# A hybrid decoder trunk on one core: first gate ahead of later weight splits, first rounds later, last conv tile by token halves

## The chip, the cores and the metric

The kernel runs on one core of one Trainium2 chip. The metric is device time in microseconds (us). The kernel before takes 1067.33 us (median of 3 runs, 1067.3 to 1068.85). TensorE is called PE, VectorE DVE, ScalarE ACT, GpSimd POOL, and SyncE, which issues most DMAs, SP. SBUF is the on-chip memory that all engines read; PSUM is the accumulator memory of PE, here eight banks of 128 x 512 floats.

## The reference

Two layers over 512 tokens of 1024 channels, in fp32. Layer A is a Conformer convolution module and a SwiGLU FFN, layer B attends over a shared K/V in a window of 128 and has an FFN too; a last RMSNorm follows. The change is about the first half of layer A (and, in one helper, about all RMSNorms):

```python
def rmsnorm(x, g):
    xf = x.astype(jnp.float32)
    xf = xf * lax.rsqrt(jnp.mean(xf * xf, axis=-1, keepdims=True) + EPS)
    return (xf * g.astype(jnp.float32)).astype(x.dtype)

def conformer_conv(x, w_pw1, b_pw1, w_dw, b_dw, ln_g, ln_b, w_pw2, b_pw2):
    a = jax.nn.glu(x @ w_pw1 + b_pw1, axis=-1)
    y = lax.conv_general_dilated(
        a, w_dw[:, None, :].astype(a.dtype), window_strides=(1,),
        padding=((CONV_WIDTH - 1, 0),),
        dimension_numbers=('NWC', 'WIO', 'NWC'),
        feature_group_count=D_MODEL) + b_dw
    y = jax.nn.silu(layernorm(y, ln_g, ln_b))
    return y @ w_pw2 + b_pw2
```

## The kernel before

Channels lie on partitions, tokens along the free dimension. An fp32 product is made of three products in a faster format: each operand is split in a high part (a cast) and a low part (the rest), and `mm3` (lines 345 to 347, in a fixed order `mm3_in_turn`, line 337) adds high·high, high·low and low·high in one bank. Weight chunks are split by ACT (`whi`) and DVE (`wlo`, both line 269). The chunks have numbers: pw1's tile ct has chunks 2·ct and 2·ct + 1, and `split_limit` and `held` say how far, and after which instruction, `split_chunk` may go.

The first stage ends at about 162 us. Its PE work is pw1 tile by tile (`project`): eight tiles ct of 128 channels, each with a linear and a gate bank and two halves of 24 products. RMSNorm's per-token factor is applied behind the product. It is made once (`Rms`): squares summed over channels, sums over partitions by PE, `ms` (DVE, line 435), `rs` by a power on POOL (line 437), then `diagonals` (DVE, line 452: identity times rs), which `spread` multiplies by a matrix of ones on PE, so that each partition has the row, and a copy to `rsbc` by ACT (line 447).

`gate` (lines 774 to 777) multiplies both banks by rsbc, takes a sigmoid and writes `apad`, the padded input of the depthwise convolution. Then SP stores apad to DRAM (`rowsd`, line 782) and loads it back four times, shifted (`shifted`, line 784). The 31 taps are shared by three engines: `products` (ACT multiplies, POOL adds, line 826), `taps` (a chain on DVE that sums in a PSUM bank, the last one into y, line 280) and `rounds` (PE products over 32-row blocks of `shifted` with diagonal `tables`, three to five rounds of four for each tile). DVE builds the tables in `round_weights` (line 712). `last` (DVE, line 843) joins PE's bank and y.

`inside(ct)` places other work between the products of tile ct: in tile 1 the sums, the spread and conv 0's gate; in tiles 2 to 5, after the first half, rounds and join of conv ct − 2. Behind the eighth tile stand the rounds of convs 4 to 6, then conv 7, which has four of its taps on PE by diagonal matrices (`diagonals` of `Conv`), then the sums for the LayerNorm (`sums`, `means`, `scales`), and the LayerNorm itself, which feeds pw2.

Banks come from a ring of eight in the order of the calls of `bank()`: a call waits for the last reader of the bank eight calls ago. `in_turn`, `Turn` and `issue_after` fix an order on an engine by hand; elsewhere a scheduler orders the instructions of each engine.

## Time and profile before

| what | value |
|---|---|
| median of three runs | 1067.33 us |
| profiled execution | 1066.32 us |
| its span | 1064.5 us |
| PE busy in the span | 1042.4 us (98%) |
| DVE, ACT, POOL busy | 71%, 47%, 17% |
| mean granted PE clock | 0.991 |
| first stage's end (first product of pw2) | 160.8 us |

Times in the trace count from the start of the span. A row of the timeline gives start and length of a run of alike instructions, engine, line and operation, the tile written and read, the shape, how many there were, and in brackets how long the engine had been idle and what ended that. A product in fp32 stands as two records, so 12 of them are x24.

### The profile page before, as it was taken

To read this page: it belongs to the slowest core of one execution; us is meant where nothing else is said; L and a number is where in the kernel's file an instruction comes from. 1 tells how busy PE (TensorE), PEld (TensorE's weight loads), DVE (VectorE), ACT (ScalarE), POOL (GpSimd) and SP (SyncE) were. 2 spreads that over 40 slices of the span, in tenths; PEclk is the share of its full clock that TensorE was granted. 3 is DMA by queue.
4 is the path that set the end of the run, shared out by engine and by line. 5 is a ranking of instruction groups with operands and counts; after the bars stand their busy time and mean duration, and the time that the engine had idled before them with its cause. 6 is when DMAs were issued, how large, how long until landed. Compare 5 with 4: busy or idle time off the path is not lost.

```text
span 1064.5 us, 15933 instructions
## 1 busy us (share of the span) xinstructions
PE 1042.4 (98%) x6404; PEld 893.5 (84%) x6404; DVE 759.7 (71%) x986; ACT 500.7 (47%) x764; POOL 182.0 (17%) x200
## 2 busy tenths in 40 slices
PE   8799999999999999999999999999999999999997
PEld 6466637888999899899988787788899988998996
DVE  7889837769786577658486767577978755776563
ACT  6565716434454254235463665354445522552353
POOL 0689810421000000000031342142100000000000
PEclk9899999999999999999999999999999999999999
DMA  7646568324234134221323211232423441243112
GB/s 252 176 141 160 139 141 118 99 84 154 80 100 159 40 106 143 89 80 61 119 79 99 80 41 41 80 99 79 139 79 102 131 145 40 99 141 97 41 60 79
DMA packets 36917, 111.62 MB, mean 105 GB/s; under 512 B 4395, under 2 KB 7260, under 8 KB 36828
## 3 DMA queue, kind: packets, MB, share of 16 engines
q1 hardware_dynamic: 35692, 109.32, 34.7%
q10 hardware_dynamic: 1152, 1.29, 0.3%
q8 instruction: 50, 0.82, 0.3%
q14 instruction: 23, 0.19, 0.1%
HBM read 106.25 MB, written 4.73 MB: 104 GB/s over the span
## 4 chain that ended last, share of the span: by engine, by line
PE 94%; DVE 2%; DMA 1%; issue 1%; ACT 1%; POOL 0%; SPq 0%; POOLq 0%; ACTq 0%; DVEq 0%
PE bank L337 24%; PE bank L345 23%; PE bank L346 23%; PE bank L347 22%; PE bank L1226 2%; DVE quad L470 1%; DMA shifted<-rowsd 1%; DVE wlo L269 0%; DMA rnd<-in_rnd_dram 0%; DVE tables L712 0%; DMA rowsd<-apad 0%; PE bank L1216 0%; PE bank L462 0%; PE bank L433 0%; ACT whi L269 0%
## 5 line engine op out<-in xcount | busy, mean ns | idle before, releaser
L346 PE MATMUL bank<-quad,whi 128*128 128x256 f32 (+1 forms) x1536 | 489.0, 320 | 1.3 <-DVE quad L470 0.9
L345 PE MATMUL bank<-quad,whi 128*128 128x256 f32 (+1 forms) x1536 | 483.2, 320 | 0.3 <-ACT tmp L617 0.3
L347 PE MATMUL bank<-quad,wlo 128*128 128x256 f32 (+1 forms) x1536 | 481.8, 319 | 0.0
L269 ACT CAST whi<-raw 128x1024 fp32r<-128x1024 f32 x174 | 182.3, 1050 | 296.6 <-PE bank L346 195.2
L346 PEld LDWEIGHTS bank<-quad,whi 128*128 128x128 f32 x1536 | 292.5, 190 | 23.5 <-DVE quad L470 1.3
L345 PEld LDWEIGHTS bank<-quad,whi 128*128 128x128 f32 x1536 | 291.2, 190 | 22.8 <-ACT quad L280 0.7
L347 PEld LDWEIGHTS bank<-quad,wlo 128*128 128x128 f32 x1536 | 290.0, 190 | 20.7 <-issue 0.5
L269 DVE TENSOR_TENSOR wlo<-raw,whi 128x1024 fp32r<-128x1024 f32 x174 | 221.3, 1275 | 110.7 <-ACT whi L269 99.6
L337 PE MATMUL bank<-quad,whi 128*128 128x512 f32 x512 | 162.3, 398 | 3.6 <-DVE quad L280 2.6
L337 PEld LDWEIGHTS bank<-quad,whi 128*128 128x128 f32 x512 | 95.6, 190 | 31.0 <-issue 5.3
L269 DVE TENSOR_TENSOR wlo<-blocks,whi 128x1024 fp32r<-128x1024 f32 x54 | 65.5, 1221 | 54.3 <-ACT whi L269 54.3
L337 PE MATMUL bank<-quad,wlo 128*128 128x512 f32 x256 | 100.3, 392 | 0.0
L269 ACT CAST whi<-blocks 128x1024 fp32r<-128x1024 f32 x54 | 56.6, 1048 | 86.8 <-PE bank L346 65.6
L826 POOL TENSOR_TENSOR quad<-quad 128x512 f32<-128x512 f32 x53 | 72.9, 1376 | 19.1 <-ACT quad L824 15.9
L337 PEld LDWEIGHTS bank<-quad,wlo 128*128 128x128 f32 x256 | 48.4, 189 | 10.4
L1237 POOL TENSOR_TENSOR rs<-ss,mhalf 128x1 f32<-128x1 f32 x4 | 2.2, 547 | 297.6 <-DVE ss L1235 297.6
L423 POOL TENSOR_TENSOR tmp<-tmp,tmp 128x512 f32<-128x512 f32 x21 | 32.9, 1566 | 113.1 <-ACT tmp L421 89.0
L1099 POOL COPY sc<-sk 128x4 f32<-128x4 f32 x16 | 3.5, 253 | 256.8 <-DVE wlo L269 254.6
L824 ACT ACTIVATE quad<-apad,wdw 128x512 f32<-128x512 f32 x53 | 36.6, 717 | 17.2 <-POOL quad L826 17.2
L499 DVE TENSOR_TENSOR h<-bank,h 128x512 f32<-128x512 f32 x56 | 37.1, 684 | 8.4 <-PE bank L347 8.4
L1123 POOL TENSOR_SCALAR sc<-sc,sm 128x256 f32<-128x256 f32 (+1 forms) x64 | 31.6, 514 | 66.0 <-DVE sm L1121 65.9
L1119 ACT ACTIVATE sc<-sc,m 128x257 f32<-128x257 f32 (+1 forms) x64 | 30.2, 475 | 22.2 <-DVE m L1110 22.2
(167 smaller groups left out, 1010.4 us busy)
## 6 DMA issues: line engine op xcount, KB each, us to landing
raw<-in_W_dram SPq DMA_DIRECT2D x139, 512.0 KB, 3.5
blocks<-in_W_dram SPq DMA_DIRECT2D x36, 512.0 KB, 4.5
shifted<-rowsd SPq DMA_DIRECT2D x16, 262.0 KB, 5.8
shifted<-rowsd SPq DMA_DIRECT2D x12, 260.0 KB, 5.3
rowsd<-apad SPq DMA_DIRECT2D x8, 271.0 KB, 2.5
bias<-fd SPq DMA_DIRECT2D x8, 256.0 KB, 10.2
h<-in_xT_dram SPq DMA_DIRECT2D x3, 512.0 KB, 7.1
shifted<-rowsd SPq DMA_DIRECT2D x4, 264.0 KB, 5.1
```

The costliest lines, as they stand in the source:

```text
L269: done = (nc.scalar.copy(hi, r).ins, lo_engine[0].tensor_sub(lo, r, f32(hi)).ins)
L337: turn[0] = nc.tensor.matmul(*args, **kw).ins
L345: nc.tensor.matmul(out, w[0], x[0], start=start, stop=False, **kw)
L346: nc.tensor.matmul(out, w[0], x[1], start=False, stop=False, **kw)
L347: nc.tensor.matmul(out, w[1], x[0], start=False, stop=stop, **kw)
L423: eng.tensor_add(sq, self.acc[eng], sq)
L499: nc.vector.tensor_add(t, banks[m], t)
L824: nc.scalar.mul(pr, src, self.tap(j))
L826: nc.gpsimd.tensor_add(to, acc, pr)
L1119: nc.scalar.activation(sc[:, j, 0:1 + w], sc[:, j, 0:1 + w], AF.Exp, bias=self.m4[:, j:j + 1], scale=-1.0, accum_out=sm[:, j:j + 1])
L1123: nc.gpsimd.tensor_scalar(sc[:, j, 1:1 + w], sc[:, j, 1:1 + w], sm[:, j:j + 1], 0.0, op0=ALU.mult, op1=ALU.add)
L1226: nc.tensor.matmul(self.banks[g], x, w[:, k, :], start=False, stop=kp == LAST[1] - 1 and k == 1 and n == 2)
```

## The change

Seven things change, all in the first stage but for the first:

1. `spread` takes the column of factors itself. Four products, each with one column repeated 128 times as the stationary side and the identity as the moving side, give what one product of ones by a diagonal matrix gave. `diagonals` and its DVE operation go, for all rms rows and for both LayerNorm rows.
2. The three tables built ahead of the first split of x are not built there. Four tables (0 to 3) are built between `ms` and the first gate, the other four after the gate of tile 1. There are nine warm-up products for seven.
3. Conv 0's gate comes ahead of the splits of chunks 5, 6 and 7, which are held until it has been issued.
4. Rounds and join of conv 0 move from the middle of tile 2 to its end; the position table and its rows move one tile later.
5. The DMAs of a gate are issued in the order of the code.
6. Conv 7 works in two banks by halves of 256 tokens: diagonal taps, rounds, join with y, copy, square and sums for each half.
7. `means` comes behind the first half's join.

On DVE, around conv 0's gate (`apad_334` before, `apad_329` after; tables, gate, and the splits `wlo` of chunks 5 to 7), before, from the row behind ms:

```order
L712 TENSOR_TENSOR tables_137<-eye,rnd 128x512
L712 TENSOR_TENSOR tables_138<-eye,rnd 128x384
L452 TENSOR_TENSOR tmp_308<-ident,rs_304 128x512
L712 TENSOR_TENSOR tables_138<-eye,rnd 128x512 x2
L712 TENSOR_TENSOR tables_138<-eye,rnd 128x640
L269 TENSOR_TENSOR wlo_322<-raw_215,whi_321 128x1024
L269 TENSOR_TENSOR wlo_438<-raw_241,whi_437 128x1024
L774 TENSOR_TENSOR tmp_336<-bank_212,rsbc_178 128x512
L776 TENSOR_TENSOR bank_211<-bank_211,rsbc_178 128x512
L774 TENSOR_TENSOR tmp_398<-bank_272,rsbc_178 128x512
L776 TENSOR_TENSOR bank_271<-bank_271,rsbc_178 128x512
L777 SCALAR_TENSOR_TENSOR apad_334<-bank_211,prm,tmp_336 128x512
```

and now:

```order
L435 TENSOR_SCALAR ms_301<-bank_296 128x4
L701 TENSOR_TENSOR tables_139<-eye,rnd 128x384
L701 TENSOR_TENSOR tables_139<-eye,rnd 128x512
L701 TENSOR_TENSOR tables_139<-eye,rnd 128x384
L701 TENSOR_TENSOR tables_139<-eye,rnd 128x512
L764 TENSOR_TENSOR tmp_331<-bank_211,rsbc_177 128x512
L766 TENSOR_TENSOR bank_210<-bank_210,rsbc_177 128x512
L764 TENSOR_TENSOR tmp_397<-bank_271,rsbc_177 128x512
L767 SCALAR_TENSOR_TENSOR apad_329<-bank_210,prm,tmp_331 128x512
L269 TENSOR_TENSOR wlo_344<-raw_214,whi_343 128x1024
L269 TENSOR_TENSOR wlo_441<-raw_240,whi_440 128x1024
L280 TENSOR_SCALAR bank_366<-apad_329,wdw 128x512
```

The line numbers are those of the changed kernel. The diagonal is gone, the tables ahead of the gate are four instead of five, and no split stands between ms and the gate. Behind it, on DVE, where conv 0's taps end and conv 1's begin, before:

```order
L280 TENSOR_SCALAR bank_367<-apad_334,wdw 128x512
L280 SCALAR_TENSOR_TENSOR bank_367<-apad_334,wdw,bank_367 128x512 x7
L280 SCALAR_TENSOR_TENSOR quad_132<-apad_334,wdw,bank_367 128x512
L280 TENSOR_SCALAR bank_423<-apad_396,wdw 128x512
L280 SCALAR_TENSOR_TENSOR bank_423<-apad_396,wdw,bank_423 128x512 x6
L280 SCALAR_TENSOR_TENSOR quad_132<-apad_396,wdw,bank_423 128x512
L269 TENSOR_TENSOR wlo_564<-raw_319,whi_563 128x1024
```

and now:

```order
L269 TENSOR_TENSOR wlo_471<-raw_272,whi_470 128x1024
L280 SCALAR_TENSOR_TENSOR bank_366<-apad_329,wdw,bank_366 128x512 x6
L280 SCALAR_TENSOR_TENSOR quad_134<-apad_329,wdw,bank_366 128x512
L280 TENSOR_SCALAR bank_422<-apad_395,wdw 128x512
L701 TENSOR_TENSOR tables_140<-eye,rnd 128x384
L701 TENSOR_TENSOR tables_140<-eye,rnd 128x512 x2
L701 TENSOR_TENSOR tables_140<-eye,rnd 128x640
L280 SCALAR_TENSOR_TENSOR bank_422<-apad_395,wdw,bank_422 128x512 x6
L269 TENSOR_TENSOR wlo_561<-raw_315,whi_560 128x1024
L280 SCALAR_TENSOR_TENSOR quad_134<-apad_395,wdw,bank_422 128x512
```

Four tables stand behind the first tap of conv 1, and a split between its last two taps. On PE, where rounds 0 stood in the middle of tile 2 (bank_434 and bank_433), before:

```order
L337 MATMUL bank_433<-quad_129,whi_275 128x512
L337 MATMUL bank_433<-quad_128,wlo_276 128x512
L337 MATMUL bank_465<-shifted_341,tables_137 32x512 x12
L337 MATMUL bank_434<-quad_130,whi_321 128x512
L337 MATMUL bank_434<-quad_131,whi_321 128x512
```

and now, between the last products of tile 2 and the first of tile 3:

```order
L337 MATMUL bank_436<-quad_132,whi_343 128x512
L337 MATMUL bank_436<-quad_133,whi_343 128x512
L337 MATMUL bank_436<-quad_132,wlo_344 128x512
L337 MATMUL bank_498<-shifted_336,tables_139 32x512 x12
L337 MATMUL bank_557<-quad_130,whi_440 128x512
L337 MATMUL bank_557<-quad_131,whi_440 128x512
```

On PE behind the last rounds of conv 6 (the sums alternate y and its square, and four rows like the two shown are left out), before:

```order
L337 MATMUL bank_1149<-shifted_1004,tables_138 32x512 x16
L337 MATMUL bank_1181<-apad_1088,quad_136 128x512 x4
L337 MATMUL bank_885<-quad_133,ones_m 32x512
L337 MATMUL bank_885<-quad_136,ones_m 32x512
L337 MATMUL bank_1197<-sel,tmp_1195 128x2 x4
L337 MATMUL bank_1181<-shifted_1095,tables_138 32x512 x16
L337 MATMUL bank_1181<-quad_133,ident 128x512
L337 MATMUL bank_1181<-shifted_1095,tables_138 32x512 x4
L337 MATMUL bank_1197<-sel,quad_133 128x1 x4
L337 MATMUL bank_1197<-sel,quad_136 128x1 x4
L337 MATMUL bank_1242<-quad_132,ones_m 128x512
```

and now:

```order
L337 MATMUL bank_1184<-apad_1091,quad_138 128x256 x4
L337 MATMUL bank_1185<-apad_1091,quad_138 128x256 x4
L337 MATMUL bank_888<-quad_135,ones_m 32x512
L337 MATMUL bank_888<-quad_138,ones_m 32x512
L337 MATMUL bank_1184<-shifted_1098,tables_140 32x256 x20
L337 MATMUL bank_1184<-quad_135,ident 128x256
L337 MATMUL bank_1226<-sel,tmp_1224 128x2 x4
L337 MATMUL bank_1226<-sel,quad_135 128x1 x2
```

```order
L337 MATMUL bank_1226<-sel,quad_138 128x1 x2
L337 MATMUL bank_1185<-shifted_1098,tables_140 32x256 x20
L337 MATMUL bank_1185<-quad_135,ident 128x256
L337 MATMUL bank_1226<-sel,quad_135 128x1 x2
L337 MATMUL bank_1226<-sel,quad_138 128x1 x2
L337 MATMUL bank_1273<-ident,mv_1265 128x128 x4
L337 MATMUL bank_1278<-quad_134,ones_m 128x512
L337 MATMUL bank_1280<-ident,rr_1268 128x128 x4
```

Each half has its own rounds, join and sums, and the `sel` products stand behind the first half's join.

```diff
-N_WARM = 7
+N_WARM = 9
...
-            had = nc.vector.tensor_scalar(ms, st[:, 0:4], 1.0 / D, EPS, op0=ALU.mult, op1=ALU.add).ins
+            self.had = nc.vector.tensor_scalar(ms, st[:, 0:4], 1.0 / D, EPS, op0=ALU.mult, op1=ALU.add).ins
             self.rs = small.tile([P, 4], F32, tag="rs", name=uid("rs"))
             nc.gpsimd.tensor_tensor(self.rs, ms, mhalf, op=ALU.pow)
-            if between is not None:
-                had = between(had)
-            with tc.issue_after(had):
-                self.diag = diagonals(self.rs)
 
         def step2(self):
             self.step1()
             if self.stage != 2:
                 self.stage = 2
-                nc.scalar.copy(self.bc, spread(self.diag, self.matmul))
+                nc.scalar.copy(self.bc, spread(self.rs, self.matmul))
...
-    def spread(diag, matmul):
+    def spread(cols, matmul):
 
         pb = bank()
-        matmul(pb, ones_m, diag, start=True, stop=True)
+        for n in range(NBLK):
+            matmul(pb[:, n * P:(n + 1) * P], cols[:, n:n + 1].to_broadcast([P, P]), ident, start=n == 0,
+                   stop=n == NBLK - 1, skip_group_check=True)
         return pb
...
 
-        dves.last = round_weights(range(3))
...
+        split_limit[0] = 5
+        copies = Turn()
...
@@ -774,16 +764,17 @@
                 nc.vector.tensor_mul(sig, self.gt, rs_bc)
                 gated = nc.scalar.activation(sig, sig, AF.Sigmoid, bias=col("b1", KT + ct)).ins
...
-                nc.vector.scalar_tensor_tensor(a[:, PAD:], self.lin, col("b1", ct), sig, op0=ALU.add, op1=ALU.mult)
+                self.gated = nc.vector.scalar_tensor_tensor(a[:, PAD:], self.lin, col("b1", ct), sig, op0=ALU.add,
+                                                            op1=ALU.mult).ins
                 n = S + 4 * (self.r - 1)
                 q = self.q = cv.tile([P, 4, S + 4 * (max(ROUNDS) - 1)], F32, tag="shifted", name=uid("shifted"), bufs=4)
                 row = PAD + S
                 ad = dpool.tile([P, row], F32, tag=uid("rows"), name=uid("rowsd"))
-                nc.sync.dma_start(ad, a)
...
             def diagonals(self):
-                self.c = bank()
-                for n in range(self.n_diag):
-                    j = TAPS - self.n_diag + n
-                    in_turn(self.c, diag[:, n, :], self.a[:, j:j + S], start=n == 0, stop=False, skip_group_check=True)
...
+
+                self.c = [bank()[:, 0:S // 2] for _ in HALF]
+                for half, tok in enumerate(HALF):
+                    for n in range(self.n_diag):
+                        j = TAPS - self.n_diag + n
+                        in_turn(self.c[half], diag[:, n, :], self.a[:, j + tok.start:j + tok.stop], start=n == 0, stop=False,
+                                skip_group_check=True)
+
+            def rounds(self, half=None):
                 if not self.n_diag:
                     self.c = bank()
+                tok, c = (slice(0, S), self.c) if half is None else (HALF[half], self.c[half])
                 w = weights_of[self.ct]
                 for n in range(self.r):
-                    if self.n_diag and n == self.r - 1:
-                        in_turn(self.c, ident, y[self.ct], start=False, stop=False, skip_group_check=True)
                     for g in range(4):
-                        in_turn(self.c[g * 32:(g + 1) * 32, :], w[:, g * self.r + n, :],
-                                self.q[:, g, 4 * n:4 * n + S], start=n == 0 and not self.n_diag, stop=n == self.r - 1,
-                                skip_group_check=True)
+                        in_turn(c[g * 32:(g + 1) * 32, :], w[:, g * self.r + n, :],
+                                self.q[:, g, 4 * n + tok.start:4 * n + tok.stop], start=n == 0 and not self.n_diag,
+                                stop=n == self.r - 1 and not self.n_diag, skip_group_check=True)
+
+            def join(self, half):
+                in_turn(self.c[half], ident, y[self.ct][:, HALF[half]], start=False, stop=True, skip_group_check=True)
...
-            nc.vector.tensor_copy(y[KT - 1], c)
+        def last_sums(b, c, half):
+
+            tok = HALF[half]
+            halves_turn(nc.vector.tensor_copy, y[KT - 1][:, tok], c[half])
             sq = next_of(1, sqs)
-            with tc.issue_after(nc.scalar.square(sq, c).ins):
-                nc.scalar.activation(warm, warm, AF.Silu)
+            silu_after.append(nc.scalar.square(sq[:, tok], c[half]).ins)
             for i, t in enumerate((y[KT - 1], sq)):
-                for n in range(NBLK):
+                for n in range(2 * half, 2 * half + 2):
                     in_turn(b[:, 2 * n + i:2 * n + i + 1], t[:, n * P:(n + 1) * P], inv_d, start=False,
                             stop=i == 1 and n == NBLK - 1)
...
+        halves_turn, silu_after = Turn(), []
+
+        def scales(b):
+
+            with tc.issue_after(silu_after[-1]):
+                nc.scalar.activation(warm, warm, AF.Silu)
             dve = Turn()
             mv, m2, var, rr = (small.tile([P, 4], F32, tag=n, name=uid(n)) for n in ("mv", "m2", "var", "rr"))
             dve(nc.vector.tensor_copy, mv, b[:, 0:8:2])
             dve(nc.vector.tensor_mul, m2, mv, mv)
             dve(nc.vector.scalar_tensor_tensor, var, b[:, 1:8:2], EPS, m2, op0=ALU.add, op1=ALU.subtract)
             nc.gpsimd.tensor_tensor(rr, var, mhalf, op=ALU.pow)
+            pm = spread(mv, in_turn)
             idle(1)
-            with tc.issue_after(dve.last):
-                pm = spread(diagonals(mv), in_turn)
-            prs = spread(diagonals(rr), in_turn)
+            prs = spread(rr, in_turn)
             idle(2)
             return pm, prs
...
                 if ct == 1 and (half, n) == (0, 5):
-                    rms0.step1(lambda after: round_weights((3, 4), after))
-                    held[0] = (round_weights((5, 6, 7), spread_of[0]),)
+                    rms0.step1()
+                    round_weights((0, 1, 2, 3), rms0.had)
                 if ct == 1 and (half, n) == (1, 1):
                     rms0.step2()
-                    convs[0].begin()
-                if half == 0 and n == 7 and 2 <= ct < KT - 2:
+                    convs[0].gate()
+                    split_limit[0] = 2 * KT
+                    held[0] = (convs[0].gated,)
+                    held[0] = (split_chunk(5)[1],)
+                    convs[0].products()
+                    convs[0].taps()
+                if half == 1 and n == 7 and ct == 2:
+                    convs[0].rounds()
+                    convs[0].last()
+                if half == 0 and n == 7 and 3 <= ct < KT - 2:
                     convs[ct - 2].rounds()
                     convs[ct - 2].last()
                 if half == 1 and n == 7:
-                    if ct == 2:
+                    if ct == 3:
                         table()
-                    if ct == 3:
+                    if ct == 4:
                         table_rows()
                     if ct == 4:
                         shift_rows()
@@ -935,18 +945,25 @@
             c.project(inside(ct))
             if ct:
                 c.begin()
+            if ct == 1:
+                round_weights((4, 5, 6, 7), c.gated)
...
-        convs[KT - 1].diagonals()
+        end = convs[KT - 1]
+        end.diagonals()
         sums(KT - 4, KT - 3)
         sums(KT - 2)
-        b = means()
-        convs[KT - 1].rounds()
-        pm, prs = scales(b, convs[KT - 1].c)
+        b = None
+        for half in range(2):
+            end.rounds(half)
+            end.join(half)
+            b = means() if b is None else b
+            last_sums(b, end.c, half)
+        pm, prs = scales(b)
```

18 lines of the change are left out of this document (5 added, 13 removed).

## The prediction

> **What bounds the kernel now.** I read the page first, then the waits, the stretches and the chain of the first stage, then the rows of the engines there. The page says that TensorE (PE) is the bound:
>
> ```profile
> span 1064.5 us, 15933 instructions
> PE 1042.4 (98%) x6404; PEld 893.5 (84%) x6404; DVE 759.7 (71%) x986; ACT 500.7 (47%) x764; POOL 182.0 (17%) x200
> ```
>
> So a change can only pay by what PE lacks: 22 us of idle time and a few microseconds at a low clock. The waits of the first 170 us (total, times, longest) show the largest piece:
>
> ```profile
> PE bank L337 <- DMA shifted<-rowsd: 7.8, 1, 7.8
> ```
>
> One wait of 7.8 us: PE stands before the first rounds until the shifted copies of conv 0 have landed. The stretches around it (length, then busy time and count of PE, PEld, DVE, ACT, POOL, then clock, DMA share, GB/s):
>
> ```profile
> 24.00:47.00 23.00, 15.18 (x69) 11.99 (x68) 20.86 (x30) 11.33 (x16) 10.63 (x9) 0.90 0.71 199
> 47.00:52.00 5.00, 4.99 (x24) 1.11 (x24) 3.40 (x5) 3.08 (x5) 4.92 (x6) 0.50 0.78 152
> 52.00:79.00 27.00, 27.00 (x134) 19.04 (x130) 20.53 (x23) 16.68 (x23) 22.68 (x18) 0.99 0.47 135
> 79.00:128.00 49.00, 49.00 (x245) 33.92 (x244) 43.33 (x50) 31.15 (x47) 45.85 (x35) 1.00 0.65 159
> ```
>
> PE is busy 15.2 of 23 us, then runs at a granted clock of 0.50, and from 52 on it never stops. DVE is busy 43.3 of 49 us in the fourth stretch: whatever PE gains, DVE must be able to follow. The chain of waits to that stop, and the rounds on PE:
>
> ```profile
> 25.92 0.17 DVE ms L435
> 26.24 1.35 POOL rs L437
> 28.22 2.02 DVE tables L712 x3
> ...
> 35.64 2.82 DMA rowsd<-apad
> ...
> 39.90 6.98 DMA shifted<-rowsd
> 47.02 5.35 PE L337 MATMUL bank<-shifted,tables 128*32 128x512 f32 x24 [7.83 <-DMA shifted<-rowsd]
> 64.61 3.64 PE L337 MATMUL bank<-shifted,tables 128*32 128x512 f32 x32
> 79.28 2.78 PE L337 MATMUL bank<-shifted,tables 128*32 128x512 f32 x24
> ```
>
> From ms through pow, tables, splits and gate to the store and the loads of conv 0 it is one chain; the two rounds of 24 records each (rounds 0 at 47.02, rounds 2 at 79.28) differ by 5.35 − 2.78 = 2.57 us, which is the low clock. After the first stage PE is the bound in both kernels and the later stages keep their order, so what the first stage gains or loses by 162 us is what the time changes by, save for three spreads (below).
>
> **The front: first gate earlier.** ms waits on PE now. PE's late start is a part of that:
>
> ```profile
> 6.18 1.63 DVE L712 TENSOR_TENSOR tables<-eye,rnd 128x384 f32<-128x384 f32 x3 [3.89 <-DMA rnd<-in_rnd_dram]
> 8.53 0.79 PE L337 MATMUL bank<-quad,whi 128*128 128x512 f32 x1 [2.65 <-DVE quad L280]
> 22.28 2.35 DVE L269 TENSOR_TENSOR wlo<-raw,whi 128x1024 fp32r<-128x1024 f32 x2
> 34.82 0.74 DVE L777 SCALAR_TENSOR_TENSOR apad<-bank,prm,tmp 128x512 f32<-128x512 f32 x1
> 28.62 1.02 PE L337 MATMUL bank<-tmp,ones_m 128*128 128x512 f32 x2
> 29.68 0.59 ACT L447 COPY rsbc<-bank 128x512 f32<-128x512 f32 x1 [1.38 <-PE bank L337]
> ```
>
> Three tables stand ahead of the first split of x and leave PE idle for 2.65 us at 8.53; now they go behind ms, and two more warm matmuls fill a bit of that gap. PE thus comes earlier to the sums, and ms is bound by DVE, which finishes splits 3 and 4 at 22.28 + 2.35 = 24.63 instead of 25.92: **−1.3**. I give DVE itself no gain there, since the later h tiles land no earlier. From ms: pow 1.35, the spread (four 128-column products instead of one 512-column one; 1.02 now, and I take 1.0), then ACT's copy of rsbc (0.59), which puts the row at 28.05, where it was 29.68 + 0.59 = 30.27. The four tables that now stand between ms and the gate take about 2.2 (1.63 for three, 0.57 for one) and end at 26.9, under pow: nothing. Then four DVE operations of 0.62 apart and apad ends at 30.55, where it was 34.82 + 0.74 = 35.5: **−5.0**: 1.3 from ms, 0.9 from the diagonal on DVE that no longer stands between pow and spread, and the rest from two splits and one operation of tile 1 that no longer stand before it. With the same store, issue and load times (11.4 us from apad to the rounds) the copies of conv 0 are there at 42.
>
> ```profile
> 38.11 0.39 PE L337 MATMUL bank<-quad,wlo 128*128 128x512 f32 x1
> 38.79 0.39 PE L337 MATMUL bank<-quad,wlo 128*128 128x512 f32 x1
> 58.18 0.81 PE L673 MATMUL bank<-tmp 33*16 33x384 f32 x2
> 94.88 3.64 PE L337 MATMUL bank<-shifted,tables 128*32 128x512 f32 x32
> ```
>
> Three products take 38.79 − 38.11 = 0.68, so one takes 0.227. PE has the spread done at 27.4, the 18 products left of tile 1 at 31.7 (4.1 and a little for hand-overs), and tile 2 (48 × 0.227 = 10.9) at 42.6. Rounds 0, moved from tile 2's middle to its end, find their copies landed 0.6 before, at full clock: 2.7, to 45.3. Tile 3 with rounds 1 (3.6) and the table's two products (0.75 from 58.18) ends at 61.4 (42.6 + 2.7 + 10.9 + 3.6 + 0.75 and 0.8 of hand-overs). The first half of tile 4 is 24 × 0.227 = 5.4. If nothing held PE here, rounds 2 would start at 67.1, not 79.28: −12.2. This is the bound from below.
>
> **What takes over: DVE and the bank of rounds 2.** Banks go round in a ring of eight. Counting the calls of `bank()` in the changed order (rounds 0 behind tile 2, table behind tile 3), rounds 2 get the bank in which DVE sums the taps of conv 2, and one bank of tile 4 is that of rounds 0, free after their join. Before, rounds 2 got the bank of the position table, free long before. So rounds 2 now wait for DVE to end conv 2's taps. DVE's rows for that sum, and POOL's beside them:
>
> ```profile
> 35.48 1.22 DVE L269 TENSOR_TENSOR wlo<-raw,whi 128x1024 fp32r<-128x1024 f32 x1
> 38.05 5.50 DVE L280 SCALAR_TENSOR_TENSOR bank<-apad,wdw,bank 128x512 f32<-128x512 f32 x7
> 45.04 4.71 DVE L280 SCALAR_TENSOR_TENSOR bank<-apad,wdw,bank 128x512 f32<-128x512 f32 x6
> 56.12 2.10 DVE L269 TENSOR_TENSOR wlo<-raw,whi 128x1024 fp32r<-128x1024 f32 x1 [5.58 <-ACT whi L269]
> 68.83 0.75 DVE L280 SCALAR_TENSOR_TENSOR quad<-apad,wdw,bank 128x512 f32<-128x512 f32 x1
> 37.16 13.34 POOL L826 TENSOR_TENSOR quad<-quad 128x512 f32<-128x512 f32 x10 [9.58 <-ACT quad L824]
> ```
>
> and, by form between 26 and 135 us (busy, mean ns), the two-input operations whose inputs both lie in SBUF:
>
> ```profile
> L858 DVE TENSOR_TENSOR quad<-quad,quad 128x512 f32<-128x512 f32 x2 | 2.5, 1291 | 1.2 <-ACT quad L856 1.2
> L712 DVE TENSOR_TENSOR tables<-eye,rnd 128x512 f32<-128x512 f32 x3 | 2.0, 683 | 0.0
> L269 DVE TENSOR_TENSOR wlo<-raw,whi 128x1024 fp32r<-128x1024 f32 x11 | 18.8, 1715 | 7.7 <-ACT whi L269 6.0 <-PE bank L337 1.6
> ```
>
> A 128x512 addition on DVE took 1291 ns while POOL was adding (at 91.98), and a table of that size took 683 with POOL idle; the split wlo took 1.22 with POOL idle and 2.10 with POOL busy. A tap or a gate operation, which reads a PSUM bank, keeps its 0.67 to 0.79. So a two-input DVE operation beside POOL's additions costs 0.6 to 0.9 more. From apad at 30.55, on DVE: splits 5 and 6, 2.35, to 32.9; first tap, second gate's two operations and one tap, 2.8, to 35.7; split 7 beside POOL, 2.05, to 37.75; the last seven taps of conv 0 (4.71 + 0.75), to 43.2; first tap of conv 1, to 43.95. Then tables 4 to 7, which ran free before (2.0 for three, 0.6 for the fourth, the rows at 28.22 and 6.18) and now stand amid POOL's additions, which start at 31 and go on past 50 with 17 additions of 1.33. Free they cost 2.4; each waiting for the running addition they cost 6.3 (0.6 more for the first, 1.1 for each other). I take 6.3, since all comparable rows beside POOL show it: to 50.25. Six taps (4.71), to 55; split 8, to 57; last tap, two gate operations and apad, to 59.9; split 9 (1.87), to 61.8; a tap and the join of rounds 0, to 63.2; seven taps (5.5), to 68.7; split 10 (2.08), to 70.8; the last tap, to **71.5**. Conv 2's taps ended at 68.83 + 0.75 = 69.6 before, so DVE is 1.9 later while PE would be earlier.
>
> [...]
>
> So PE waits at tile 4 for the join of rounds 0 (61.4 to 63.2, about 1.7), ends the first half of it at 68.7, and waits 2.8 for rounds 2, which start at 71.5 instead of 79.28: **−7.8**. Bounds: 67.1 to 68.7 if nothing is slowed (−12.2 to −10.6), 73 if each of the eight two-input operations on the way loses 0.2 more (−6.3). These stops are shorter than the 7.83 that was followed by half clock, and I let PE keep its full clock. [...]
>
> **From rounds 2 to the tail.** PE then needs what it needed before: 15.6 to rounds 3 (94.88 − 79.28), giving 87.1, and so on:
>
> ```profile
> 128.33 9.65 PE L337 MATMUL bank<-shifted,tables 128*32 128x512 f32 x88
> 145.07 1.05 PE L337 MATMUL bank<-sel,tmp 128*128 128x2 f32 x8 [0.68 <-ACT tmp L882]
> 146.05 3.64 PE L337 MATMUL bank<-shifted,tables 128*32 128x512 f32 x32
> 152.63 1.95 PE L337 MATMUL bank<-sel,quad 128*128 128x1 f32 x16 [0.88 <-DVE quad L890]
> 156.69 0.69 DVE L452 TENSOR_TENSOR tmp<-ident,rr 128x512 f32<-128x512 f32 x1 [0.92 <-POOL rr L903]
> 159.21 0.69 DVE L280 TENSOR_TENSOR tmp<-tmp,bank 128x512 f32<-128x512 f32 x1 [0.58 <-PE bank L337]
> ```
>
> For that DVE has to make up 9.7 (7.8 + 1.9). Of its idle 5.7 in the fourth stretch and 1.6 ahead of it most is used, so apad of conv 7 comes only some 5.4 earlier, at 124.6. Its copies (10 us) are there at 134.6, the sums of PE end at 144.4 − 7.8 = 136.6: 2 us of slack, and some 0.7 at rounds 3 (their bank is that of conv 3's taps, done at 86.4). These are hidden, but thinly.
>
> **The tail by halves.** From the end of the sums (145.07 − 0.68 = 144.4) to the first multiply by rr (159.21) it took 14.8: the wait and `sel` products 1.7, rounds and joins 5.7, copy and wait 0.9, sums 2.0, moments, pow, diagonal and spread 4.6. Now: rounds of half 0 2.25, join 0.46, `sel` 1.0 (while DVE copies and ACT squares half 0), sums 1.0, half 1 2.7, its copy 0.7, sums 1.0, then 3.3 for moments, pow and spread, as the diagonal (0.69 and its hand-over) is gone. That is 12.4: **−2.5**. Bounds: 0 if the smaller pieces cost PE as much in hand-overs, −3.5 if the half sums and the copies hide wholly.
>
> **The other spreads.** Three more rms rows lose a DVE diagonal and get four products for one; PE is the bound there and has other work, so I put 0.1 each: **+0.3**, bounds −1 (the diagonal was waited for) and +1.
>
> **Sum** against the profiled execution (1066.32, of which the span is 1064.5): −7.8 − 2.5 + 0.3 = −10.0, so 1056.3; the median of the runs stands 1.0 above that execution, so **1057.3**.
>
> **Rivals.** (1) DVE is not slowed: tables cost 2.4, rounds 2 start at 67.1 and PE runs through, −12.2 − 2.5 + 0.3 = −14.4: 1053. For it: DVE and POOL need not meet at every operation; against it: all 11 splits between 26 and 135 us averaged 1.72 instead of 1.22. (2) The same mechanism, but dearer: rounds 2 at 73, behind a stop of 4.3 us that is followed by half clock as at rounds 0: −6.3 + 2.57 − 2.5 + 0.3 = −5.9; with copies of conv 7 that come late and take half of the tail's gain, −4.7: 1062. For it: the thin slacks above; against it: the price of 1291 ns is the largest of its kind already. (3) The wait only moves: the eight two-input operations (split 7, four tables, splits 8, 9 and 10) lose 0.7 to 1.0 more each, rounds 2 start at 77 to 79, and the tail's gain goes to copies of conv 7 that are late: no change, 1067. Against it: no row shows a table-sized operation above 1.3. (4) Slower: each of these eight waits for two additions of POOL in place of one (another 1.3 each), rounds 2 start past 81.8, the clock falls after a stop of 13 us, and the convs behind it are as late: +2.5 or more, 1070. It decides once DVE ends conv 2's taps after 79.3; the mean split of 1.72 beside POOL speaks against it.
>
> **How the numbers follow.** The forecast gets 0.50, rival (1) 0.20, (2) 0.20, (3) and (4) 0.05 each. About 0.2%, 2.1 us, is what can be told from no change here, so faster is 0.50 + 0.20 + 0.20 = 0.90, same 0.05, slower 0.05. The range goes from just below rival (1), 1052.5, to just above (2), 1062.5.
>
> **What would show it.** Right: apad of conv 0 at about 30.5 and its copies landed before PE ends tile 2, rounds 0 in 2.8 with no wait; a wait of PE of 1 to 4 us at rounds 2, named for DVE's tap; tables of 128x512 above 1.0 us; sums to multiply in about 12.4. Wrong: rounds 2 at 67 with no wait, rounds 0 still waiting for the copies, a wait on conv 7's copies, or a half clock behind a new stop.

## The result and the profile after

The changed kernel takes 1057.72 us (median of four runs, 1056.17 to 1058.94) against 1067.32: 9.6 us less, a ratio of 0.9908 with a 95% interval of 0.989 to 0.9925. The forecast was 1057.3. The profiled execution took 1058.01 us with a span of 1056.2, 8.3 less than the span before. (That pair understates the difference: this execution is 0.3 above its median, that of before 1.0 below.)

The page after, top and engines:

```profile
span 1056.2 us, 16105 instructions
PE 1040.7 (99%) x6494; PEld 900.2 (85%) x6494; DVE 757.9 (72%) x981; ACT 501.8 (48%) x765; POOL 185.5 (18%) x200
```

The rounds on PE, in the timeline of the kernel after (start, length, how many, and in brackets the stop ahead of them and what ended it):

```profile
41.80 2.78 PE L337 MATMUL bank<-shifted,tables 128*32 128x512 f32 x24
50.50 3.64 PE L337 MATMUL bank<-shifted,tables 128*32 128x512 f32 x32 [0.24 <-issue]
69.06 4.33 PE L337 MATMUL bank<-shifted,tables 128*32 128x512 f32 x24 [2.61 <-DMA shifted<-rowsd]
87.42 3.64 PE L337 MATMUL bank<-shifted,tables 128*32 128x512 f32 x32 [1.15 <-DVE wlo L269]
120.87 9.65 PE L337 MATMUL bank<-shifted,tables 128*32 128x512 f32 x88
```

Rounds 0 start at 41.80 with no stop and in 2.78 us: the stop of 7.83 and the half clock behind it are gone. Rounds 2 start 10.2 earlier than before (69.06 for 79.28), but behind a stop of 2.61, and they take 4.33 where 2.78 would do. Rounds 3 stop for 1.15 and start 7.46 earlier. From there the distance stays: the last block of rounds (convs 4 to 6) starts at 120.87 for 128.33, again 7.46 earlier. On DVE (start, length, line, operation, count):

```profile
24.13 0.16 DVE L435 TENSOR_SCALAR ms<-bank 128x4 f32<-128x4 f32 x1
29.33 0.74 DVE L767 SCALAR_TENSOR_TENSOR apad<-bank,prm,tmp 128x512 f32<-128x512 f32 x1
34.83 1.22 DVE L269 TENSOR_TENSOR wlo<-raw,whi 128x1024 fp32r<-128x1024 f32 x1
42.03 6.28 DVE L701 TENSOR_TENSOR tables<-eye,rnd 128x384 f32<-128x384 f32 x4
57.92 0.75 DVE L767 SCALAR_TENSOR_TENSOR apad<-bank,prm,tmp 128x512 f32<-128x512 f32 x1 [0.19 <-ACT tmp L765]
68.05 0.73 DVE L280 SCALAR_TENSOR_TENSOR quad<-apad,wdw,bank 128x512 f32<-128x512 f32 x1
```

ms at 24.13, apad of conv 0 at 29.33 + 0.74 = 30.07, then four tables in 6.28 us, apad of conv 2 at 58.67 and the end of conv 2's taps at 68.78. Rounds 2 start 0.28 after that last tap. The trace names the copies of conv 2 as what ended the stop; a hand-over from DVE to PE takes 0.06 in e2 below, so the copies came a fifth of a microsecond behind the taps: two chains, both from conv 2's apad, end at nearly the same time.

Where the rest went is seen in two stretches (length, busy time and count of PE, PEld, DVE, ACT, POOL, then clock, DMA share, GB/s) and in DVE's first multiply by rr:

```profile
66.00:74.00 8.00, 5.39 (x29) 1.65 (x29) 7.57 (x9) 4.20 (x8) 7.75 (x6) 0.79 0.49 120
147.30:150.50 3.20, 3.20 (x12) 2.17 (x11) 0.69 (x1) 0.00 (x0) 0.34 (x1) 0.51 1.11 151
150.71 0.69 DVE L280 TENSOR_TENSOR tmp<-tmp,bank 128x512 f32<-128x512 f32 x1 [2.63 <-PE bank L337]
```

The tail of before for comparison (the same columns), and the diagonal taps of conv 7 on PE, before and after:

```profile
155.20:158.60 3.40, 3.35 (x5) 1.09 (x5) 1.93 (x3) 0.00 (x0) 1.41 (x1) 0.50 0.94 131
137.91 3.70 PE L337 MATMUL bank<-apad,quad 128*128 128x512 f32 x8
130.45 3.72 PE L337 MATMUL bank<-apad,quad 128*128 128x256 f32 x16
```

The granted clock is 0.79 in the first stretch, and 0.51 in the tail from 147.3 to 150.5, much as it was before (0.50 from 155.2 to 158.6). From the diagonal taps of conv 7 to the multiply it takes 150.71 − 130.45 = 20.26, before 159.21 − 137.91 = 21.30: 1.04 less. So the span's −8.3 is −7.46 at rounds 3, −1.04 in the tail and 0.2 behind it.

### The profile page after: what moved, and what is told of

Read it like the earlier page. It is cut to its first block, busy times and chain, and to the rows that moved or that the text cites. A ratio compares the mean times of both kernels' runs of the same rounds, so it can differ in the third digit from the quotient of the medians.

```text
span 1056.2 us, 16105 instructions
## 1 busy us (share of the span) xinstructions
PE 1040.7 (99%) x6494; PEld 900.2 (85%) x6494; DVE 757.9 (72%) x981; ACT 501.8 (48%) x765; POOL 185.5 (18%) x200
## 4 chain that ended last, share of the span: by engine, by line
PE 88%; DVE 2%; issue 1%; ACT 1%; POOLq 0%; POOL 0%; ACTq 0%
PE bank L345 23%; PE bank L346 23%; PE bank L347 23%; PE bank L337 18%; PE bank L1243 2%; DVE quad L459 1%; DVE wlo L269 1%; ACT whi L269 0%; PE bank L450 0%; PE bank L1233 0%; PE bank L433 0%; DVE h L488 0%; DVE quad L280 0%; ACT tmp L280 0%; ACT quad L280 0%
## 5 line engine op out<-in xcount | busy, mean ns | idle before, releaser
L822 POOL TENSOR_TENSOR quad<-quad 128x512 f32<-128x512 f32 x53 | 77.2, 1458 | 11.5 <-ACT quad L820 8.3
```

The costliest lines, as they stand in the source:

```text
L822: nc.gpsimd.tensor_add(to, acc, pr)
```

## The experiments

All of them are compared with the kernel before, run on the same chip between them. Medians are in us, ratios go with their 95% intervals. The kernel before had medians from 1067.1 to 1068.2 beside them, so that two versions that were not run side by side are told apart to about 1 us; where median and ratio give different sizes, both are named.

| run | edit | median | ratio to before |
|---|---|---|---|
| the change | | 1057.72 | 0.9908 (0.989 to 0.9925) |
| e1 | tables early | 1056.13 | 0.9892 (0.9879 to 0.9906) |
| e2 | position table back | 1060.58 | 0.9932 (0.9919 to 0.9946) |
| e3 | rounds 2 later | 1059.85 | 0.9925 (0.9913 to 0.9938) |
| e4 | rounds 0 at the old place | 1059.22 | 0.9922 (0.9908 to 0.9935) |
| e5 | e1, and the rows' broadcast later | 1052.97 | 0.985 (0.9837 to 0.9864) |
| e6 | e5, and idle products in the tail | 1053.3 | 0.9854 (0.9841 to 0.9868) |
| e7 | before, with the tail by halves alone | 1066.24 | 0.9983 (0.9972 to 0.9994) |
| e8 | the change with conv 7 whole | 1060.18 | 0.9916 (0.9902 to 0.9931) |
| e9 | the change with the old spreads | 1058.75 | 0.9912 (0.9898 to 0.9925) |
| e10 | the change with two splits ahead of the gate | 1058.6 | 0.9904 (0.9888 to 0.9919) |
| e11 | before, with rounds 0 later alone | 1063.83 | 0.9958 (0.9945 to 0.9971) |
| e12 | the change, the rows' broadcast later | 1056.44 | 0.9904 (0.9888 to 0.9921) |

### The tables beside POOL, and what rounds 2 wait for (e1)

```diff
                 dves(nc.vector.tensor_sub, lo, r, f32(hi))
+            if k == 1:
+                dves.last = round_weights(range(3), dves.last)
...
-                    round_weights((0, 1, 2, 3), rms0.had)
+                    round_weights((3, 4, 5, 6, 7), rms0.had)
...
-            if ct == 1:
-                round_weights((4, 5, 6, 7), c.gated)
```

> Tables 0 to 2 built in DVE's pause behind the second split of x (about 7 us), tables 3 to 7 between ms and the first gate (under pow, spread and the copy of the row), none beside POOL's additions. Theory A (the four tables amid POOL's additions cost DVE 6.3 us and put apad of conv 2, its copies and its taps late, and so make PE stop 2.6 us at rounds 2 and lose another 1.5 us to half clock behind it): apad of conv 2 about 3 us earlier, rounds 2 at 66.5 with no stop and in 2.8 us, rounds 3 about 4 earlier unless their copies bind, time about 1053.5 (4 us below the changed kernel). Rival B (the copies of conv 2 come late for reasons of the DMA queues, the tables are hidden): rounds 2 still at about 69, time 1057.5. Rival C (the five tables delay the first gate by more than they save): apad of conv 0 later than 30.5, time 1058 or more.

The same tables by form on DVE, of the kernel after (between 26 and 135 us: busy, mean ns) and then of e1 (from 0 to 135):

```profile
L701 DVE TENSOR_TENSOR tables<-eye,rnd 128x512 f32<-128x512 f32 x3 | 4.2, 1410 | 0.0
L701 DVE TENSOR_TENSOR tables<-eye,rnd 128x640 f32<-128x640 f32 x1 | 1.9, 1915 | 0.0
L701 DVE TENSOR_TENSOR tables<-eye,rnd 128x384 f32<-128x384 f32 x1 | 1.1, 1051 | 0.0
```

```profile
L701 DVE TENSOR_TENSOR tables<-eye,rnd 128x512 f32<-128x512 f32 x4 | 2.6, 682 | 0.0
L701 DVE TENSOR_TENSOR tables<-eye,rnd 128x640 f32<-128x640 f32 x1 | 0.8, 816 | 0.0
L701 DVE TENSOR_TENSOR tables<-eye,rnd 128x384 f32<-128x384 f32 x3 | 1.7, 551 | 0.0
```

The same instruction took 682 ns where POOL made no additions and 1410 amid them, 816 and 1915, 551 and 1051. That is the price that the forecast put on them. And PE in e1:

```profile
67.37 2.78 PE L337 MATMUL bank<-shifted,tables 128*32 128x512 f32 x24 [0.67 <-DVE quad L280]
85.65 5.34 PE L337 MATMUL bank<-shifted,tables 128*32 128x512 f32 x32 [2.63 <-DVE wlo L269]
```

Rounds 2 start 1.7 earlier, behind a stop of 0.67 and at full clock: Theory A's first half. But the median is only 1.6 lower where 4 were expected, and even that is not shown to come from the tables. Rounds 3 now stop for 2.63 and then run at half clock (5.34 for 3.64), and the last block of rounds in e1 starts where it did after the change (120.87):

```profile
120.80 9.65 PE L337 MATMUL bank<-shifted,tables 128*32 128x512 f32 x88
```

So the wait moved on to the next pair of copies and took nearly the whole gain (ms came 0.4 later in this execution, too); the 1.6 by which the two profiled spans differ is the tail's clock, which was full in this execution of e1 (see the part on the tail).

### Copies of conv 3 behind a broadcast (e5, e12)

```diff
-            nc.sync.dma_start(fd.rearrange("q h k -> q (h k)"), f1.to_broadcast([16, NH * 3 * P]))
+            copies(nc.sync.dma_start, fd.rearrange("q h k -> q (h k)"), f1.to_broadcast([16, NH * 3 * P]))
...
-                    if ct == 4:
+                    if ct == 5:
                         table_rows()
```

e5 has this edit on top of e1's, e12 has it alone.

> The early tables of the first experiment, and the broadcast of the position table's rows moved one tile later and behind conv 4's copies in SP's queue, so that it no longer stands ahead of conv 3's store. With the early tables alone rounds 2 started at 67.4, but rounds 3 then stood 2.6 us for their copies (13.4 us after their apad, where conv 2's took 10.3) and ran at half clock (5.34 for 3.64). Theory F (the rows' broadcast made conv 3's copies late, and this stop is where the gain went): copies 10.4 us after apad, rounds 3 at about 83 with no stop over 0.5 us and at full clock, time 1056.1 - 4.3 = 1052. Rival G (weight loads in the same queue make them late as well): rounds 3 at 85 or later, time 1055 to 1056. Rival H (the gain goes on to the tail: conv 7's copies late): rounds 3 at 83, but a stop ahead of conv 7's rounds, time 1054 to 1056.

> The changed kernel with one edit: the broadcast of the position table's rows one tile later and behind conv 4's copies in SP's queue. If that broadcast made conv 3's copies late (and not DVE, which the trace names at rounds 3): the stop of 1.15 us ahead of rounds 3 goes, time 1056.5. Rounds 2 keep their stop of 2.6 at about 69. If DVE holds rounds 3: stop and time stay, 1057.7.

SP's DMA issues of the kernel after, and then of e5 (start, length, line, tiles, count):

```profile
74.06 0.57 SPq L668 DMA_DIRECT2D fd<-f  x1
74.72 0.52 SPq L248 DMA_DIRECT2D raw<-in_W_dram  x1
75.34 0.38 SPq L280 DMA_DIRECT2D rowsd<-apad  x1
80.24 1.75 SPq L280 DMA_DIRECT2D shifted<-rowsd  x4
```

```profile
72.28 0.34 SPq L280 DMA_DIRECT2D rowsd<-apad  x1
76.34 1.75 SPq L280 DMA_DIRECT2D shifted<-rowsd  x4
87.78 0.57 SPq L280 DMA_DIRECT2D fd<-f  x1
```

After the change, the broadcast (fd) and a weight load go ahead of conv 3's store, which is issued 1.6 us after its apad was ready (73.71) and needs 4.9 us until the loads go out. With fd behind conv 4's loads (e5) the store is issued at 72.28, 0.06 after its apad, and the loads go out 4.1 later, at 76.34. Rounds 2, rounds 3 and the last block of rounds of e5, and then rounds 3 of e12:

```profile
67.78 2.78 PE L337 MATMUL bank<-shifted,tables 128*32 128x512 f32 x24 [0.45 <-DVE quad L280]
83.80 3.64 PE L337 MATMUL bank<-shifted,tables 128*32 128x512 f32 x32 [0.36 <-issue]
117.24 9.65 PE L337 MATMUL bank<-shifted,tables 128*32 128x512 f32 x88
```

```profile
86.12 3.64 PE L337 MATMUL bank<-shifted,tables 128*32 128x512 f32 x32
```

In e12 the stop of 1.15 is gone (the row has no bracket); the median is 1.3 lower, where 1.2 was expected, though by the ratio it is only 0.4 (the kernel before ran at 1067.09 there), so the time alone would not show it. In e5 rounds 3 stop for 0.36 and run at full clock, and the time is 1052.97: Theory F within 1 us. This version beats both kernels, the change by 4.8 us (6 by the ratio); 3.6 of that are seen at the last block of rounds (117.24 for 120.87), where e1 alone brings 0.1 and e12 alone 1.3 (119.57). The two edits are worth more together, as each alone leaves the other's wait. The trace had named DVE's split as what ended the stop at rounds 3; moving a DMA removed it.

### The ring of banks (e2)

```diff
-                    if ct == 3:
+                    if ct == 2:
                         table()
-                    if ct == 4:
+                    if ct == 3:
                         table_rows()
```

> Position table at the end of tile 2 and its rows at the end of tile 3, as in the kernel before; all else as changed. Rounds 2 then no longer share a bank with conv 2's taps. If the bank alone held rounds 2: they start when PE arrives, 66.5, and the time falls by 4 us to 1053.5. If the copies of conv 2 hold them too (they landed within 0.3 us of the end of the taps): rounds 2 stay at 69. If the stop of 1.15 us at rounds 3 came from the broadcast of the position table's rows, which stood ahead of the store of conv 3 in SP's queue: that stop goes, and the time falls by 1.1 us to 1056.6; if it came from DVE, which the trace names: it stays.

The result is on the other side: 1060.58, 2.9 slower than the change. Rounds 1 on PE, and DVE's last tap of conv 1:

```profile
57.08 5.64 PE L337 MATMUL bank<-shifted,tables 128*32 128x512 f32 x32 [5.57 <-DVE quad L280]
56.29 0.73 DVE L280 SCALAR_TENSOR_TENSOR quad<-apad,wdw,bank 128x512 f32<-128x512 f32 x1
```

With the table's bank taken in tile 2, rounds 1 are the eighth call behind the bank of conv 1's taps, and they start 0.06 after the last of these (57.02), behind a stop of 5.57 and at half clock. I had counted the ring for rounds 2 and not for rounds 1. So the mechanism (rounds wait for DVE's taps through the ring) is shown, at another place than expected, and the question about rounds 2 and 3 was not answered by this run; e12 answered that of rounds 3.

### Where rounds 2 and rounds 0 stand (e3, e4, e11)

e3 places rounds 2, e4 rounds 0:

```diff
 e3
-                if half == 1 and n == 7 and ct == 2:
-                    convs[0].rounds()
-                    convs[0].last()
-                if half == 0 and n == 7 and 3 <= ct < KT - 2:
+                if half == 1 and n == 7 and ct in (2, 4):
+                    convs[ct - 2].rounds()
+                    convs[ct - 2].last()
+                if half == 0 and n == 7 and ct in (3, 5):
 e4
-                if half == 1 and n == 7 and ct == 2:
-                    convs[0].rounds()
-                    convs[0].last()
-                if half == 0 and n == 7 and 3 <= ct < KT - 2:
+                if half == 0 and n == 7 and 2 <= ct < KT - 2:
```

> Rounds and join of conv 2 at the end of tile 4 instead of its middle; all else as changed. PE then does the second half of tile 4 (5.4 us) while the copies land. Theory A: no stop and no half clock there, rounds 2 at about 72 in 2.8 us, rounds 3 at 83 plus what their own copies make them wait (these were there only at 87.4): the gain of 4 us is then taken back by a longer stop of up to 4 us at rounds 3, time 1055 to 1058. Rival: rounds 3 wait less, as their copies were late only through PE: 1053.5.

> Rounds and join of conv 0 back in the middle of tile 2; the early gate stays. Theory A (the move was needed, since the copies land only at about 41): PE stops at 36.4 for about 4.5 us, rounds 0 run at half clock (2.5 us more), and of that the stop at rounds 2 (2.6 and 1.5 for the clock) is saved: about +3, 1060.5. Rival D (the stop at rounds 2 absorbs it, the move brings nothing): 1057.5. Rival E (all of it counts): 1064.5.

e11 is the kernel before with only this move and the position table one tile later:

> The kernel before with one part of the change alone: rounds and join of conv 0 at the end of tile 2, and the position table one tile later (else rounds 1 would get the bank of conv 1's taps); gate, tables, spreads and tail as before. Theory P (most of the gain is the move, as PE has tile 2's second half to do while the copies land): rounds 0 at 47.0 behind a stop of 2.4 instead of 7.8, rounds 2 at 72.3 for 79.3, time -7: 1060.5. Rival Q (a stop of 2 to 3 us at rounds 2 or 3 or half clock takes part of it): -4, 1063.5. Rival S (without the early gate it brings nothing): 1067.5.

Rounds 2 and 3 of e3, then rounds 0 and 2 of e4, then rounds 0 and 3 of e11:

```profile
72.40 2.78 PE L337 MATMUL bank<-shifted,tables 128*32 128x512 f32 x24
87.70 5.43 PE L337 MATMUL bank<-shifted,tables 128*32 128x512 f32 x32 [5.13 <-DMA shifted<-rowsd]
```

```profile
41.49 4.48 PE L337 MATMUL bank<-shifted,tables 128*32 128x512 f32 x24 [4.43 <-DVE bank L280]
72.69 2.78 PE L337 MATMUL bank<-shifted,tables 128*32 128x512 f32 x24
```

```profile
49.05 2.78 PE L337 MATMUL bank<-shifted,tables 128*32 128x512 f32 x24 [2.51 <-DMA shifted<-rowsd]
91.75 5.34 PE L337 MATMUL bank<-shifted,tables 128*32 128x512 f32 x32 [2.74 <-DVE wlo L269]
```

In e3 the stop at rounds 2 is gone and comes back twice as long (5.13) at rounds 3, with half clock: 1059.85, 2.1 slower than the change and past my range of 1055 to 1058, as I had not counted the half clock. In e4 PE stops for 4.43 and rounds 0 run at half clock; most of it is saved at rounds 2, which have no stop there (72.69): +1.5, between Theory A (+3) and D. In e11 the move alone is worth 4.2 us, Rival Q: its stop at rounds 0 is 2.51, but one of 2.74 at rounds 3 with half clock gives part of it back. So the move alone makes 4.2 of the 9.6, and without the move 8.5 are left (1067.72 − 1059.22): the parts are worth less together than one by one. That fits that each takes away the same idle time of PE ahead of conv 0's copies: 7.83 before, 4.43 in e4, 2.51 in e11, none with both.

### The gate ahead of the splits, and the spreads (e10, e9)

e10 lets chunks 5 and 6 be split ahead of the gate again; e9 puts the diagonals back:

```diff
 e10
-        split_limit[0] = 5
...
-                    round_weights((0, 1, 2, 3), rms0.had)
+                    held[0] = (round_weights((0, 1, 2, 3), rms0.had),)
...
-                    convs[0].gate()
-                    split_limit[0] = 2 * KT
-                    held[0] = (convs[0].gated,)
-                    held[0] = (split_chunk(5)[1],)
-                    convs[0].products()
-                    convs[0].taps()
+                    convs[0].begin()
 e9
+            with tc.issue_after(self.had):
+                self.diag = diagonals(self.rs)
...
-                nc.scalar.copy(self.bc, spread(self.rs, self.matmul))
+                nc.scalar.copy(self.bc, spread(self.diag, self.matmul))
...
-            pm = spread(mv, in_turn)
             idle(1)
-            prs = spread(rr, in_turn)
+            with tc.issue_after(dve.last):
+                pm = spread(diagonals(mv), in_turn)
+            prs = spread(diagonals(rr), in_turn)
```

> The changed kernel with the splits of chunks 5 and 6 ahead of the first gate again, the rest as changed (rounds 0 at the end of tile 2). Theory M (only DVE's total work up to conv 2's apad and taps counts, which is the same; the early gate alone brings little): copies of conv 0 2.3 later, a stop of PE of about 2 us at rounds 0, and as much less at rounds 2, which still start at 69: 1057.7, at most +1.5 for a second half clock. Rival N (the lead of the gate counts in full): rounds 2 at 71.3, time 1060.

> The changed kernel with the spreads as before (diagonal on DVE, one product of ones by it), the rest as changed; the diagonal of the first row stands on DVE behind the four tables. By the prediction's terms: apad of conv 0 and all behind it on DVE 0.9 to 1.4 later, so rounds 2 at 70.1 to 70.5; the tail 1.3 longer; the other spreads 0.3 back: 1059.6 to 1060.1. Rival: the first row's share is hidden by PE's stop elsewhere, only the tail counts: 1058.7. Rival: the new spread costs as much on PE as it saves: 1057.7.

Rounds 0, 2 and 3 of e10, then the first spread and rounds 2 of e9:

```profile
42.12 2.78 PE L337 MATMUL bank<-shifted,tables 128*32 128x512 f32 x24
70.05 2.78 PE L337 MATMUL bank<-shifted,tables 128*32 128x512 f32 x24 [3.14 <-DMA shifted<-rowsd]
87.90 3.64 PE L337 MATMUL bank<-shifted,tables 128*32 128x512 f32 x32 [2.15 <-issue]
```

```profile
27.35 1.12 PE L337 MATMUL bank<-tmp,ones_m 128*128 128x512 f32 x2 [1.09 <-DVE tmp L450]
70.29 4.08 PE L337 MATMUL bank<-shifted,tables 128*32 128x512 f32 x24 [2.77 <-DMA shifted<-rowsd]
```

In e10 apad of conv 0 comes 1.4 later (31.51), not 2.3, as DVE had stood idle for 1.1 ahead of the gate, and rounds 0 still do not stop, at 42.12. The stops at rounds 2 and 3 are longer (3.14 and 2.15) but not followed by half clock. The median is 0.9 above the change, by the ratio 0.4 below it. So the gate's lead over two splits, on which the forecast spent a good part of its −5.0, is not clear of zero in the time. Conv 2's apad ends at 59.07, 0.4 later than after the change, as ms does (24.49 for 24.13): the work of DVE up to there is the same in either order, which speaks for Theory M. But rounds 2 start at 70.05, between M's 69 and N's 71.3, and this execution was spared the half clock there, which cost 1.55 after the change: its stop lay across two of the clock's steps, with 1.92 and 1.22 us (last part); so the run leaves the lead's worth open. In e9 the first spread waits 1.09 for the diagonal and rounds 2 come 1.2 later, as forecast, and the last block of rounds 1.5 later (122.39). The median is 1.0 higher (0.4 by the ratio) instead of the 1.9 to 2.4 expected; in the profile the tail, which kept its clock (next part), takes 0.7 less than that of the change.

Two parts of the change have no run of their own: the tables that no longer stand ahead of the first split, and the order of the DMAs. The first is likely to count. In the three profiled executions with the old front (before, e7, e11) the first tables started when their input `rnd` had landed, at 6.18, 7.33 and 7.76, and ms came at 25.92, 28.20 and 27.84, each time behind a wait for PE. In the eleven with the new front ms came between 24.13 and 24.76. So the front gains 1.8 us at ms in the pair of profiles shown above, and up to 4 against other executions of the old one. This may also be why the medians differ by more than that pair does.

### The tail (e7, e8, e6)

e7 takes over from the change `Conv.diagonals`, `rounds`, `join`, `last_sums`, `scales` and the loop over the halves, with the old spreads; e8 undoes the same in the changed kernel. e6 adds idle products to e5:

```diff
             b = means() if b is None else b
+            if half:
+                idle(1)
...
+            idle(1)
             pm = spread(mv, in_turn)
```

> The kernel before with the tail by halves alone (diagonal matrices, spreads and everything else as before). The prediction's sum for the tail was -2.5, of which 1.2 by the halves and 1.3 by the diagonal that is gone; so here -1.2, 1066.3 against 1067.5, and sums to multiply by rr in 13.6 for 14.8. Rival: hand-overs and half clock eat it, 1067.5; or the whole 2.5 is the halves', 1065.

> The changed kernel with conv 7 whole again (new spreads, early gate and the rest stay). By the prediction's sum the halves are worth 1.2: 1058.9. Rival: nothing, 1057.7; or the whole tail gain, 1060.2.

> As the one before, with an idle product on PE ahead of each of the two waits of the tail (copy of the second half, moments). In the profile of the changed kernel PE ran at 0.50 from 147.3 to 150.5, in that of the early tables it did not, and conv 7's rounds to the first multiply by rr took 14.6 and 13.0 us. Theory K (the clock falls because of small products and short stops there, and a filled stop keeps it): full clock to the end of the tail, 13 us, and 0 to 1.6 us below the kernel before in this list, with less spread among its runs. Rival L (the idle products stand in the way and the clock falls just as often): same or 0.5 us slower.

The halves alone are worth 2.0 us by the medians of e7 (ratio 0.9983, 0.9972 to 0.9994), and undoing them costs 2.5 by those of e8 (0.9 by the ratio), whose five runs lie between 1057.4 and 1062.3. The profiles tell the parts better, by the time from the diagonal taps of conv 7 to the multiply by rr. Six of the fourteen kept full clock there: e1 18.69 (149.07 − 130.38) and e12 18.70 (halves and new spreads), e7 19.59 and e9 19.58 (halves, old spreads), e8 19.87 (whole, new spreads), and e6 (below). So at full clock the halves bring 1.2 and the spreads 0.9. The kernel before with 21.30 (e11 21.47) and the change with 20.26 (e2, e3, e4, e5 and e10 up to 20.36) had half clock at the end. The stretch of e1 that answers to the change's 147.3 to 150.5:

```profile
146.00:149.00 3.00, 2.87 (x19) 2.39 (x20) 1.09 (x4) 0.72 (x2) 1.03 (x1) 1.00 0.71 109
```

Clock 1.00 there and 0.51 in the change, with the same code in the tail: the half clock came in some executions and not in others (what went with it is in the last part), and made 1.6 us (20.26 for 18.69), more than either part of the edit. Whether e6's idle products prevent it isn't settled: its profiled tail kept full clock and took 19.19, 0.5 more than e1's; its runs lie within 0.7 us where e5's lie within 1.9, but its median is no lower.

## Why the prediction was right

The forecast was 1057.3, the measured time 1057.72, and what kept PE from running through (−14.4) was in the main what was named: DVE, slowed beside POOL, makes conv 2 late, and PE stops at rounds 2. That the number came so close is in part luck, as the steps show:

- **The front.** Right: ms at 24.13 (forecast 24.63), apad of conv 0 at 30.07 (30.55), rounds 0 at 41.80 behind tile 2 with no stop (42.6). How much of the −5.0 at that apad counts stays open: e10 gives 1.4 of it back, and the time rises by 0.9, which is not clear of zero. The place of rounds 0 counts (e4, e11), and so, by e10's apad of conv 2, does DVE's total up to there rather than its order. The −1.3 at ms was 1.8, and old fronts that started later would have made it more (above).
- **The tables beside POOL.** Right: 6.28 for 6.3, and e1 shows that it is their neighbour that costs. The digit is luck: the forecast's own terms for the free tables (2.0 and 0.6) make 2.6 and not the 2.4 that it used (e1's four take 2.7), and the surcharge was smaller than taken.
- **What holds rounds 2.** Half right: a stop, as forecast, of 2.61 for 2.8, but at 69.06 for 71.5. DVE ended conv 2's taps at 68.78, since three of the splits on the way kept a short time (split 7 took 1.22, not 2.05; splits 9 and 10 1.23 and 1.47): beside split 7 it was POOL's addition, begun 0.12 behind it, that took 2.24 instead of 1.3, beside split 9 POOL made none, and beside split 10 the running one ended 0.38 after the split's start; and the copies of conv 2 came as late as the taps, which the sum didn't list as a bound. By the distances the named cause, the tap by way of the ring, never ended last: in the change and the seven other profiles with its places for rounds and table (e1, e5, e6, e8, e9, e10, e12), rounds 2 start 0.13 to 0.88 behind the last tap, more than the hand-over of 0.06, and 10.3 to 11.0 behind conv 2's apad, though the trace names the tap in e1 and e5. Both chains start at that apad, so the forecast lost little by naming the other one. The ring is shown by e2 (at rounds 1), not by rounds 2 themselves. The stop of 1.7 forecast at tile 4 did not come.
- **The clock behind the stop.** Wrong. "These stops are shorter than the 7.83 that was followed by half clock, and I let PE keep its full clock": after 2.61 us rounds 2 took 4.33 for 2.78, 1.55 us. That is rival (2)'s mechanism on the forecast's stop, and one of the signs that the prediction named for being wrong. The trace of before could have told: its stop of 2.65 us, ahead of the product at 8.53, was followed by half clock too (0.50 from 8.41 to 11.82); whether so short a stop cost anything here went with its place (last part).
- **Rounds 3.** Wrong by 1.15: the slack of 0.7 was counted against the taps alone, and SP's queue was not walked through. The position table's rows, moved one tile later by the same change, stood ahead of conv 3's store (e12).
- **The copies of conv 7.** Right: no stop; apad at 122.6 (124.6).
- **The tail.** Right in kind, too large in size: at full clock 1.2 for the halves (e8 against e1) and 0.9 for the spreads (e7 against e1) are 2.1 of the 2.5, and in this pair of profiles it was 1.04. From the end of the sums to the multiply it took 14.6 (150.71 − 136.13) where 12.4 was forecast and named as a sign of being right; e1, at full clock, took 13.0. The half clock at the end stayed and makes 1.6 of that; the sum had taken 12.4 for the new tail at full clock and compared it with an old one at half clock.
- **The sum.** −10.0 came close to −9.6 partly since errors met: rounds 2 were 2.4 better than forecast, the clock and the broadcast took 2.7 back, and of the tail's term 1.0 came in the profile. The medians differ by 1.3 more than the two profiled executions do, which no term foresaw: by the profiles it is −8.3. The +0.3 for the other spreads fits the 0.2 that is left behind the tail, though nothing isolates it. A slip of 0.3 (61.4 and 5.4 make 66.8, not 67.1) touches only the bound from below.

Rival (1), DVE not slowed, fell with the tables' durations; (3) and (4) fell with rounds 2 at 69.06.

## What to carry to other kernels

When a stop of the bound engine is taken away, walk every chain that ends at its next meeting point (copies, taps, banks, and the DMA queue with all that stands in it), because several of them can end within a few tenths of a microsecond of each other; here a further 5 us (e5) came from two that the change had made late itself, and either alone brought 0.1 to 1.3 in the profiles. A small table on VectorE beside GpSimd's additions cost twice its time here (1410 ns for 682 at 128x512), so it belongs in a pause of VectorE that is there anyway. A move that passes work from one tile to the next also turns the ring of buffers: count it for every later user, not only for the one in question.
